# Mixture-of-experts stage of a two-layer encoder: activations turned earlier, the last jobs queued earlier, and row sums with the ones as stationary operand

## The chip, the core and the metric

The kernel runs on one core of one Trainium2 chip. The metric is the device time of one execution in microseconds (us); lower is better. The engines have short names in the profile: PE is the matrix engine (PEld its weight loads), DVE the vector engine, ACT the scalar engine, POOL the general-purpose one, SP the one whose queue issues the weight transfers.

## The reference, cut to what matters

Two trunk layers run on 256 prompt rows and 32 sample rows (288 in all) of width 1024. The change touches only the last step of the second layer: eight experts, of which each row uses two, and the layer norm behind them.

```python
def swiglu(h, wg, wu, wd):
    return (jax.nn.silu(h @ wg) * (h @ wu)) @ wd

def moe_swiglu(h, w_router, wg, wu, wd):
    logits = (h @ w_router).astype(jnp.float32)
    top_val, top_idx = lax.top_k(logits, TOP_K)
    top_w = jax.nn.softmax(top_val, axis=-1)
    combine = jnp.sum(jax.nn.one_hot(top_idx, N_EXPERTS, dtype=jnp.float32) * top_w[..., None], axis=-2)
    out = jnp.zeros_like(h)
    for e in range(N_EXPERTS):          # wg, wu: 1024 x 3584, wd: 3584 x 1024, float32
        out = out + combine[..., e:e + 1] * swiglu(h, wg[e], wu[e], wd[e])
    return out
...
f = moe_swiglu(h, W['w_router'][i], W['w_exp_gate'][i], W['w_exp_up'][i], W['w_exp_down'][i])
x = layer_norm(ALPHA * x + g2 * f, W['ln_g'][l, 1], W['ln_b'][l, 1])
```

## The kernel before, in words

The experts are sorted by the number of their rows (rank r, 0 the fullest). Four are HEAVY (ranks 0, 2, 1, 3 in this order) and four LIGHT (5, 4, 6, 7). A heavy expert has a block of 128 rows (kind "F", computed in three products of a high and a low float32r part); ranks 0 and 1 also have a block of 32 (kind "N", plain float32). A light expert has only an N block, of 64 rows for rank 4 and of 32 for the others. Every expert is worked in four pieces of its 3584 hidden columns (1024, 1024, 1024, 512), and each piece has three phases: `gate`, `up` and `down`. Pieces are counted over all experts of a stream, 0 to 15, so heavy piece 15 is the last of rank 3 and light piece 15 the last of rank 7. The list `phases` fixes one order of all 96 phases, heavy and light in turn; within a stream it goes gate of piece i, down of piece i - 1, up of piece i. Five light phases stand at the end: up of 14, gate of 15, down of 14, up of 15, down of 15.

Weights come in units of 1 MB through a ring of nine buffers (`raw`), in the order of the phases; a transfer is issued by SP as soon as its buffer is given back (L134). For F blocks each half of a unit is split: ACT casts it to `whi` (L158), DVE subtracts to `wlo` (L162). N blocks read `raw` directly, with stationary tiles of 32 or 64 columns, four or two side by side on the array.

Phases touch three PSUM banks named `gu`. A gate or up phase of an F piece takes one for each 512 columns, that of a light N piece takes one, and a bank is free again when the Silu (L1410, L1438) or the product (L1412, L1440) has read it. The N block of a heavy expert uses the bank `ex` instead. `turn` transposes the finished activations of a piece on PE into `gu` banks (L1462) and copies them out, as `hFh` (ACT, L1466) and `hFl` (DVE, L1467) for F, as `tNH` or `tNL` for N (L1335, by ACT and DVE in alternation). `down` multiplies them with the down weights (F: L1490, N: L1510).

Small jobs are Python generators in a list `work`; `filler()` runs one step of the first. They are called after each unit of a light phase, after each unit of an F-only down, and once after each phase. The jobs are `fetch` and `place` (the rows of the next expert), `scatter` (the weighted result of an expert back to all 288 rows, eight steps, L1548 on PE and L1315 on DVE into `xT`), and for the end `gates` (the norm's weights and the gate of the last expert's rows, L1568 to L1579) and `rows`. `rows` first forms the row sums of `xT` (L1591), then `row` transposes `xT` to natural order into the banks of the base (L1607). `before`, called ahead of the very last unit, runs what is left in `work` and does the last two `row`; `finish` adds the last expert and does the layer norm and the stores.

Of the kernel before, what the change touches and what calls it, by code (L numbers as in the profile page):

```python
# [8 lines left out]
F32 = mybir.dt.float32  # L9
# [8 lines left out]
P = 128  # L18
# [189 lines left out]
def body(tc, I, O, CST):  # L208
# [1109 lines left out]
    def experts():  # L1318
        with tc.tile_pool(name="msplit", bufs=4) as ms_pool, tc.tile_pool(name="mw", bufs=2) as mw, \
# [63 lines left out]
            def up(name, stream, at):  # L1383


                r, (c0, n) = stream[at]
                units = n * D // (2048 * P)
                per = 2048 // n
                both = len(UNITS[r]) > 1
                for i, (kind, _, m) in enumerate(UNITS[r]):  # L1390
                    if kind == "F":
                        pss = [gu() for _ in range(n // 512)]
                        xh, xl = X[r, i]
                        for h in range(units):
                            for g in range(2):
                                hi, lo = mring.get((name, r, c0, h), g, AHEAD)
                                for k in range(per // 2):
                                    kk = per * h + per // 2 * g + k
                                    for o, (x, w) in enumerate(((xh, hi), (xl, hi), (xh, lo))):
                                        for c, ps in enumerate(pss):  # L1400
                                            TE.matmul(ps, x[:, kk, :], w[:, k, 512 * c:512 * (c + 1)], start=kk + o == 0,  # L1401
                                                      stop=kk == KT - 1 and o == 2)
                            if not both:
                                ahead()
                        if name == "gate":
                            H[r, c0, i] = mw.tile([P, 1024], F32, name="sg")[:, 0:n]
                        for c, ps in enumerate(pss):
                            d = H[r, c0, i][:, 512 * c:512 * (c + 1)]
                            if name == "gate":
                                S.activation(d, ps, AF.Silu)  # L1410
                            else:
                                V.tensor_mul(d, d, ps)  # L1412
                        continue
                    wd = n * m // P
                    if not both:
                        ps = gu()[:, 0:wd]
                    else:
                        if name == "gate":
                            H["ex"] = acc("ex")
                        ps = H["ex"][:, 0:wd] if name == "gate" else H["ex"][:, wd:2 * wd]  # L1420
                    for h in range(units):
                        w = mring.held((name, r, c0, h)) if both else mring.get_raw((name, r, c0, h))
                        for k in range(per):
                            kk = per * h + k
                            for g in range(P // m):
                                TE.matmul(ps[g * m:(g + 1) * m, :], X[r, i][:, kk, :], w[:, k, g * wd:(g + 1) * wd],  # L1426
                                          start=kk == 0, stop=kk == KT - 1)
                        if both:
                            mring.done_held((name, r, c0, h))
                        else:  # L1430
                            mring.done_raw()
                        ahead()
                        if not both:
                            filler()
                    if name == "gate":
                        d = mw.tile([P, 256], F32, name="hNH") if both else mw.tile([P, 512], F32, name="hNL")
                        H[r, c0, i] = d = d[:, 0:wd]
                        S.activation(d, ps, AF.Silu)  # L1438
                    else:
                        V.tensor_mul(H[r, c0, i], H[r, c0, i], ps)  # L1440
# [32 lines left out]
            def down(stream, at):  # L1473
# [8 lines left out]
                for i, (kind, _, m) in enumerate(UNITS[r]):  # L1482
                    if kind == "F":
                        for h in range(units):
                            for g in range(2):
                                q = 2 * h + g
                                hi, lo = mring.get(("down", r, c0, h), g, AHEAD)
                                for o, (x, w) in enumerate(((hs[i][0], hi), (hs[i][1], hi), (hs[i][0], lo))):
                                    for c in range(2):
                                        TE.matmul(DN[r, i][c], x[:, q, :], w[:, 0, 512 * c:512 * (c + 1)], start=first and q + o == 0,  # L1490
                                                  stop=final and q == 2 * units - 1 and o == 2)
                            if not both:
                                ahead()
                                filler()
                        continue
                    wd = n * m // P
                    nu = max(wd // 256, 1)
                    for h in range(units):
                        if final and r == LIGHT[-1] and h == units - 1:
                            before()  # L1500
                        w = mring.held(("down", r, c0, h)) if both else mring.get_raw(("down", r, c0, h))
                        for k in range(2):
                            if wd == P:
                                x = hs[i][:, m * (2 * h + k):m * (2 * h + k) + m]
                            else:
                                a = P * (2 * (h % nu) + k) + m * (h // nu)
                                x = hs[i][:, a:a + m]
                            for c in range(2):
                                a = 64 * c + k * m % 64
                                TE.matmul(DN[r, i][0][a:a + m, :], x, w[:, k, 512 * c:512 * (c + 1)],  # L1510
                                          start=first and h == 0 and k * m < 64, stop=final and h == units - 1 and (2 - k) * m <= 64)
                        if both:
                            mring.done_held(("down", r, c0, h))
                        else:
                            mring.done_raw()
                        ahead()
                        filler()
                if final and r == LIGHT[-1]:
                    finish(*W.pop((r, 0)), DN[r, 0][0])
                elif final:  # L1520
# [14 lines left out]
                        ys.append((kind, yh, yl, back))  # L1535
                    work.append(scatter(ys))
                    if len(W) == 1 and LIGHT[-1] == next(iter(W))[0]:
                        work.extend((gates(), rows()))

            def scatter(ys):  # L1540
                yield
# [42 lines left out]
            def rows():  # L1584

                st = last["st"] = mw.tile([P, 20], F32, name="stats", bufs=1)
                t = gu()
                for b in (0, 2, 1):
                    t0, n = BLK[b]
                    for k in range(KT):  # L1590
                        TE.matmul(t[0:n, b:b + 1], xT[:, k, t0:t0 + n], ones[:, 0:1], start=b + k == 0, stop=b == 1 and k == KT - 1)  # L1591
                    if b != 1:
                        yield
                V.tensor_scalar(st[:, 16:18], t[:, 0:2], -1.0, None, op0=ALU.mult)
                V.tensor_scalar(st[0:NSA, 18:19], t[0:NSA, 2:3], -1.0, None, op0=ALU.mult)
                yield
                tags = iter(("dF0", "dF1", "dNH", "ex"))
                for b, (t0, n) in enumerate(BLK[:2]):
                    for c in range(2):
                        base[b, c] = acc(next(tags))  # L1600
                        row(b, c)
                        yield

            def row(b, c):
                t0, n = BLK[b]
# [74 lines left out]
            placing = {r: place(r) for r in (HEAVY[0], LIGHT[0])}  # L1680
            following = {**dict(zip(HEAVY, HEAVY[1:])), **dict(zip(LIGHT, LIGHT[1:]))}
            mring.split_to(2)
            for stream, name, at in phases:
                r, c = stream[at]
                if name == "down":
                    turn(stream, at)
                    down(stream, at)
                else:
                    if name == "gate" and c[0] == 0:
                        run_all(placing.pop(r))  # L1690
                    up(name, stream, at)
                filler()
                nxt = following.get(r)
                if nxt is not None and name == "up":
                    if c == PIECES[-2]:
                        work.append(fetch(nxt))
                    elif c == PIECES[-1]:
                        placing[nxt] = place(nxt)
                        work.append(placing[nxt])

    def dense():

# [109 lines left out]
```

## Time and profile before

| | us |
|---|---|
| median of three runs | 1861.44 (1860.39 to 1862.31) |
| the profiled execution, its own time | 1866.27 |
| its span, first to last instruction | 1864.5 |
| PE busy in it | 1743.5 (94%) |
| DVE busy | 1017.8 (55%) |
| ACT busy | 790.6 (42%) |

In the span 525.91 MB go through the DMA queues, 506.76 MB of them through SP's. A share of busy time is a mean over stages with different limits; which engine ends a stage is read from that stage. A DMA share of 1.00 or slightly more in a stretch means that all 16 DMA engines were busy throughout. The granted clock (PEclk) of 1.00 is 2.4 GHz, 0.50 is 1.2 GHz.

### The profile page before, as it was taken

The numbers are of one execution on the slowest core, as the hardware profiler recorded it, in microseconds if no ns is written. First come the engines' busy times: TensorE is split into PE (matmuls) and PEld (weight loads), VectorE is DVE, ScalarE is ACT, GpSimd is POOL, SyncE is SP. The second block draws the span as 40 slices with busy tenths as digits, with TensorE's granted clock in tenths as the row PEclk, the third lists the DMA queues.
The fourth block names the chain that finished last, engine by engine and source line by source line (L and its number), as shares of the span: only waits on it lengthen the run. The fifth ranks groups of instructions, "written<-read, shape, count | busy, mean of one in ns | idle before, by whom it ended". The sixth has DMA issues, their size and how long they took to land. (4 is left out here: it accounts for less than half of the span.)

```text
span 1864.5 us, 31193 instructions
## 1 busy us (share of the span) xinstructions
PE 1743.5 (94%) x12510; PEld 1353.1 (73%) x12510; DVE 1017.8 (55%) x1713; ACT 790.6 (42%) x1230; POOL 140.3 (8%) x176
## 2 busy tenths in 40 slices
PE   7999999899997999998799999999999998999885
PEld 4898889799996988896566665666666665676544
DVE  3446666644445556566445455755555654676432
ACT  1544454434434444453344434445344433454321
POOL 1400100400005101001200000000000000000000
PEclk9999999999998999989799999999999999999896
DMA  9665564685445455631889999999978899999992
GB/s 312 214 216 194 188 206 137 211 276 192 159 158 174 150 194 207 199 131 50 310 338 410 397 399 403 366 381 412 397 297 318 341 403 399 401 411 413 409 409 101
DMA packets 211831, 525.91 MB, mean 282 GB/s; under 512 B 9405, under 2 KB 113062, under 8 KB 198626
## 3 DMA queue, kind: packets, MB, share of 16 engines
q1 hardware_dynamic: 205588, 506.76, 72.7%
q0 software_dynamic: 5680, 16.44, 2.5%
q8 instruction: 100, 1.64, 0.4%
q10 hardware_dynamic: 414, 0.66, 0.1%
q14 instruction: 49, 0.40, 0.1%
HBM read 514.54 MB, written 9.30 MB: 281 GB/s over the span
## 5 line engine op out<-in xcount | busy, mean ns | idle before, releaser
L162 DVE TENSOR_TENSOR wlo<-raw,whi 128x1024 fp32r<-128x1024 f32 x532 | 631.6, 1219 | 305.4 <-ACT whi L158 291.0
L158 ACT CAST whi<-raw 128x1024 fp32r<-128x1024 f32 x532 | 539.1, 1044 | 347.2 <-DMA raw<-in_w_exp_up 78.5
L570 PE MATMUL mm<-hh,whi 128*128 128x288 f32 x888 | 278.2, 313 | 0.8 <-ACT uF L866 0.8
L572 PE MATMUL mm<-hh,wlo 128*128 128x288 f32 x888 | 265.1, 299 | 1.2 <-DVE wlo L162 1.2
L571 PE MATMUL mm<-hl,whi 128*128 128x288 f32 x888 | 265.5, 299 | 0.0
L570 PEld LDWEIGHTS mm<-hh,whi 128*128 128x128 f32 x888 | 169.0, 190 | 24.6 <-issue 14.8
L572 PEld LDWEIGHTS mm<-hh,wlo 128*128 128x128 f32 x888 | 168.6, 190 | 1.9 <-DVE wlo L162 1.9
L571 PEld LDWEIGHTS mm<-hl,whi 128*128 128x128 f32 x888 | 169.2, 190 | 0.3
L1426 PE MATMUL gu<-raw,xNL 128*32 128x256 f32 (+3 forms) x1792 | 137.9, 393 | 4.2 <-DMA raw<-in_w_exp_gate 1.8
L1401 PE MATMUL gu<-whi,xFM 128*128 128x512 f32 x448 | 130.2, 406 | 5.5 <-ACT whi L158 3.2
L1401 PE MATMUL gu<-whi,xFH 128*128 128x512 f32 x448 | 130.6, 407 | 0.9 <-DVE xT L1315 0.8
L1401 PEld LDWEIGHTS gu<-whi,xFM 128*128 128x128 f32 x448 | 85.1, 193 | 33.8 <-issue 6.5
L1401 PEld LDWEIGHTS gu<-whi,xFH 128*128 128x128 f32 x448 | 85.2, 193 | 28.7 <-issue 6.3
L1426 PEld LDWEIGHTS gu<-raw,xNL 128*32 128x32 f32 (+1 forms) x1792 | 63.2, 117 | 58.8 <-issue 30.1
L1490 PE MATMUL dF<-whi,hFh 128*128 128x512 f32 x224 | 76.7, 425 | 8.9 <-ACT hFh L1466 8.8
L1510 PE MATMUL dNL<-raw,tNL 128*32 128x512 f32 (+1 forms) x448 | 67.6, 607 | 13.9 <-DVE tNL L1335 7.8
L1490 PE MATMUL dF<-whi,hFl 128*128 128x512 f32 x224 | 76.9, 427 | 3.8 <-DVE hFl L1467 3.6
L1401 PE MATMUL gu<-wlo,xFM 128*128 128x512 f32 x224 | 75.1, 405 | 0.6 <-DVE wlo L162 0.5
L1401 PE MATMUL gu<-wlo,xFH 128*128 128x512 f32 x224 | 74.6, 403 | 0.0
L1490 PE MATMUL dF<-wlo,hFh 128*128 128x512 f32 x224 | 73.8, 412 | 0.0
L571 PE MATMUL lg<-hl,whi 128*128 128x288 f32 x216 | 64.5, 298 | 0.0
L572 PE MATMUL lg<-hh,wlo 128*128 128x288 f32 x216 | 64.2, 297 | 0.0
(505 smaller groups left out, 2688.8 us busy)
## 6 DMA issues: line engine op xcount, KB each, us to landing
raw<-in_w_exp_gate SPq DMA_DIRECT2D x112, 1024.0 KB, 12.8
raw<-in_w_exp_up SPq DMA_DIRECT2D x112, 1024.0 KB, 12.0
raw<-in_w_exp_down SPq DMA_DIRECT2D x112, 1024.0 KB, 13.9
raw<-in_w_ada SPq DMA_DIRECT2D x48, 1024.0 KB, 7.4
raw<-in_w_in SPq DMA_DIRECT2D x44, 1024.0 KB, 5.6
raw<-in_w_ffn_gate SPq DMA_DIRECT2D x11, 1024.0 KB, 5.1
raw<-in_w_ffn_up SPq DMA_DIRECT2D x11, 1024.0 KB, 7.7
raw<-in_w_attn_up SPq DMA_DIRECT2D x8, 1024.0 KB, 6.7
```

Source lines behind the costliest of these rows:

```text
L158: self.nc.scalar.copy(hv, raw)
L162: eng.tensor_sub(lv, raw, hv.bitcast(F32))
L570: TE.matmul(ps, hi[:, s[0], s[1]], xh, start=first, stop=False)
L571: TE.matmul(ps, hi[:, s[0], s[1]], xl, start=False, stop=False)
L572: TE.matmul(ps, lo[:, s[0], s[1]], xh, start=False, stop=last)
L1401: TE.matmul(ps, x[:, kk, :], w[:, k, 512 * c:512 * (c + 1)], start=kk + o == 0, stop=kk == KT - 1 and o == 2)
L1426: TE.matmul(ps[g * m:(g + 1) * m, :], X[r, i][:, kk, :], w[:, k, g * wd:(g + 1) * wd], start=kk == 0, stop=kk == KT - 1)
L1490: TE.matmul(DN[r, i][c], x[:, q, :], w[:, 0, 512 * c:512 * (c + 1)], start=first and q + o == 0, stop=final and q == 2 * units - 1 and o == 2)
L1510: TE.matmul(DN[r, i][0][a:a + m, :], x, w[:, k, 512 * c:512 * (c + 1)], start=first and h == 0 and k * m < 64, stop=final and h == units - ...
```

## The change

Four edits, all within the expert stage. `turn` is no longer called at the start of a down phase but up to two phases ahead of it, as soon as the piece's up phase is behind (for most pieces, directly behind the gate phase of the next piece of its stream). `gates` is queued behind the up phase of the last heavy piece instead of behind the last scatter. While only one block is left to be scattered (`len(W) == 1`), two fillers run per light unit. The row sums take the ones as stationary operand (32 columns, four tiles side by side) and `xT` as the moving one; three small products then add up the four partial sums; `row(0, 0)` stands between.

```diff
@@ up(), a light N piece, after each unit (and the same in down())
                         if not both:
                             filler()
+                            if len(W) == 1:
+                                filler()
@@ down(), behind the scatter of a heavy expert
                     if len(W) == 1 and LIGHT[-1] == next(iter(W))[0]:
-                        work.extend((gates(), rows()))
+                        work.append(rows())
@@ rows()
                 st = last["st"] = mw.tile([P, 20], F32, name="stats", bufs=1)
                 t = gu()
+                for k in range(KT):
+                    g = k % 4
+                    TE.matmul(t[32 * g:32 * g + 32, 0:T], ones[:, 0:32], xT[:, k, :], start=k < 4, stop=k >= 4)
+                sums = mw.tile([P, 1024], F32, name="sg")[:, 0:T]
+                S.copy(sums, t[:, 0:T])
+                yield
+                tags = iter(("dF0", "dF1", "dNH", "ex"))
+                base[0, 0] = acc(next(tags))
+                row(0, 0)
+                yield
+                t = gu()
                 for b in (0, 2, 1):
                     t0, n = BLK[b]
-                    for k in range(KT):
-                        TE.matmul(t[0:n, b:b + 1], xT[:, k, t0:t0 + n], ones[:, 0:1], start=b + k == 0, stop=b == 1 and k == KT - 1)
-                    if b != 1:
-                        yield
+                    TE.matmul(t[0:n, b:b + 1], sums[:, t0:t0 + n], cst[:, C_COMB:C_COMB + 1], start=b == 0, stop=b == 1)
                 V.tensor_scalar(st[:, 16:18], t[:, 0:2], -1.0, None, op0=ALU.mult)
                 V.tensor_scalar(st[0:NSA, 18:19], t[0:NSA, 2:3], -1.0, None, op0=ALU.mult)
-                yield
-                tags = iter(("dF0", "dF1", "dNH", "ex"))
-                for b, (t0, n) in enumerate(BLK[:2]):
-                    for c in range(2):
-                        base[b, c] = acc(next(tags))
-                        row(b, c)
-                        yield
+                for b, c in ((0, 1), (1, 0), (1, 1)):
+                    base[b, c] = acc(next(tags))
+                    row(b, c)
+                    yield
@@ the loop over the phases
-            for stream, name, at in phases:
+            turned = set()
+            for i, (stream, name, at) in enumerate(phases):
                 r, c = stream[at]
                 if name == "down":
-                    turn(stream, at)
                     down(stream, at)
...
+                if stream is heavy and name == "up" and at == len(heavy) - 1:
+                    work.append(gates())
+                for s, what, j in phases[i + 1:i + 3]:
+                    if what == "down" and s[j] not in turned and (s, "up", j) not in phases[i + 1:i + 3]:
+                        turned.add(s[j])
+                        turn(s, j)
```

**Place 1: PE, in the second heavy expert (rank 2).** PE's order before, from the gate phase of light piece 6 (`raw`, stationary `xNL`) over the transposes of heavy piece 5 to its down phase:

```order
L1401 MATMUL gu<-wlo,xFM_10793 128x512 x2
L1426 MATMUL gu<-raw_9011,xNL 64x512 x4
L1426 MATMUL gu<-raw_9012,xNL 64x512 x4
L1426 MATMUL gu<-raw_60,xNL 64x512 x4
L1426 MATMUL gu<-raw_61,xNL 64x512 x4
L1462 MATMUL gu<-cst,sg 128x128 x8
L1490 MATMUL dF_11390<-whi,hFh 128x512
L1490 MATMUL dF_11391<-whi,hFh 128x512
```

PE's order of the change at the same place (line 1464 is the transpose, 1492 the down product):

```order
L1401 MATMUL gu<-wlo,xFM_10793 128x512 x2
L1464 MATMUL gu<-cst,sg 128x128 x8
L1426 MATMUL gu<-raw_9011,xNL 64x512 x4
L1426 MATMUL gu<-raw_9012,xNL 64x512 x4
L1426 MATMUL gu<-raw_60,xNL 64x512 x4
L1426 MATMUL gu<-raw_61,xNL 64x512 x4
L1492 MATMUL dF_11390<-whi,hFh 128x512
L1492 MATMUL dF_11391<-whi,hFh 128x512
```

The eight transposes have moved from between the light gate phase and the heavy down phase to directly behind the heavy phase; four light units now lie between them and the products that read them.

**Place 2: PE, the last weights.** PE's order before, from the last unit of down of light piece 14 on (`raw_9012` and `raw_60` are the two units of up of piece 15, `raw_61` and, behind these rows, `raw_62` those of its down):

```order
L1510 MATMUL dNL<-raw_9011,tNL 32x512 x4
L1579 MATMUL gu<-xFM_15740,xFM_15741 64x512 x2
L1591 MATMUL gu<-ones,xT 128x1 x8
L1426 MATMUL gu<-raw_9012,xNL 32x128 x16
L1591 MATMUL gu<-ones,xT 32x1 x8
L1426 MATMUL gu<-raw_60,xNL 32x128 x16
L1591 MATMUL gu<-ones,xT 128x1 x8
L1607 MATMUL dF_15837<-cst,xT 128x128 x4
L1462 MATMUL gu<-cst,hNL 128x128
L1510 MATMUL dNL<-raw_61,tNL 32x512 x4
L1607 MATMUL dF_15850<-cst,xT 128x128 x4
L1607 MATMUL dNH<-cst,xT 128x128 x4
```

PE's order of the change, first the gate phase of light piece 15 (its units are `raw_62` and `raw_63`) with the new row sums (1594, 1605) and the rows (1616):

```order
L1594 MATMUL gu<-xT,ones 32x288 x8
L1464 MATMUL gu<-cst,hNL 128x128 x2
L1426 MATMUL gu<-raw_62,xNL 32x128 x16
L1616 MATMUL dF_15753<-cst,xT 128x128 x4
L1605 MATMUL gu<-cst,sg 128x1
L1605 MATMUL gu<-cst,sg 32x1
L1605 MATMUL gu<-cst,sg 128x1
L1616 MATMUL dF_15764<-cst,xT 128x128 x4
L1426 MATMUL gu<-raw_63,xNL 32x128 x16
L1616 MATMUL dNH<-cst,xT 128x128 x4
L1616 MATMUL ex<-cst,xT 128x128 x4
```

and then, directly behind these (three like the first of these rows stand between), the last weights:

```order
L1512 MATMUL dNL<-raw_9011,tNL 32x512 x4
L1426 MATMUL gu<-raw_9012,xNL 32x128 x16
L1426 MATMUL gu<-raw_60,xNL 32x128 x16
L1464 MATMUL gu<-cst,hNL 128x128
L1512 MATMUL dNL<-raw_61,tNL 32x512 x4
L1616 MATMUL gu<-cst,xT 32x128 x8
L1512 MATMUL dNL<-raw_62,tNL 32x512 x4
```

The last product of `gates`, the row sums and the four rows of the prompt have moved from behind the down phase of piece 14 to ahead of it; the rows of the sample (32x128) have stayed.

**Place 3: ACT, the last heavy piece.** ACT's order before, from the Silu of light gate phase 14 on (`raw_60` and `raw_9009`, `raw_9010` are weights of heavy piece 15; `hFh` is the copy for its down phase):

```order
L1438 ACTIVATE hNL<-gu 128x256
L158 CAST whi<-raw_60 128x1024 x2
L158 CAST whi<-raw_9009 128x1024 x2
L1466 CAST hFh<-gu 128x512
L158 CAST whi<-raw_9010 128x1024 x2
L1532 ACTIVATE yhF<-dF_14612,wFM 128x512
L1532 ACTIVATE yhF<-dF_14613,wFM 128x512
```

ACT's order of the change there (`xFM` are the tiles in which `gates` keeps its operands):

```order
L1440 ACTIVATE hNL<-gu 128x256
L158 CAST whi<-raw_60 128x1024 x2
L1468 CAST hFh<-gu 128x512
L1335 COPY xFM_15554<-gu 2x512
L158 CAST whi<-raw_9009 128x1024 x2
L1335 COPY xFM_15555<-gu 2x128
L158 CAST whi<-raw_9010 128x1024 x2
L1536 ACTIVATE yhF<-dF_14612,wFM 128x512
L1536 ACTIVATE yhF<-dF_14613,wFM 128x512
```

The copy `hFh` has moved ahead of the cast of the down weights `raw_9009`; a small copy of `gates` now stands behind that cast.

## Rows read from the trace of the kernel before

**Rows 1.** The page, 40 equal slices of 46.6 us, DMA engines' busy share in tenths.

```profile
DMA  9665564685445455631889999999978899999992
```

**Rows 2.** Busy time by stretch (us): PE, PEld, DVE, ACT, POOL, then PEclk, DMA share, GB/s.

```profile
1180.00:1350.00 170.00, 166.84 (x766) 104.47 (x763) 98.19 (x121) 76.64 (x89) 2.69 (x3) 0.99 1.00 389
1350.00:1510.00 160.00, 155.71 (x1127) 100.05 (x1127) 88.89 (x112) 70.33 (x83) 0.00 (x0) 1.00 0.84 329
1510.00:1780.00 270.00, 249.08 (x1767) 171.10 (x1767) 153.49 (x181) 120.70 (x140) 2.98 (x4) 0.95 1.02 407
1780.00:1820.00 40.00, 31.69 (x271) 17.02 (x269) 15.03 (x30) 6.86 (x10) 0.00 (x0) 0.96 1.02 408
```

**Rows 3.** Chain that ended last, 1819 us to the last down product: start, length, what.

```profile
1819.52 1.00 PE gu L1579 x4
1820.52 2.31 PE gu L1591 x16
1822.83 1.84 PE gu L1426 x30
1824.68 0.75 PE gu L1591 x14
...
1827.24 3.50 PE gu L1591 x16
1830.74 1.92 PE dF L1607 x8
...
1833.25 1.94 PE dNL L1510 x8
1835.19 2.01 PE dF L1607 x8
1837.20 1.71 PE dNH L1607 x8
1838.90 0.93 PE ex L1607 x8
1839.83 1.76 PE gu L1607 x15
1841.59 1.06 PE dNL L1510 x6
```

**Rows 4.** Busy time by stretch around the last landing and from there to the end.

```profile
1820.00:1843.00 23.00, 22.17 (x181) 18.07 (x177) 0.96 (x5) 2.07 (x3) 0.00 (x0) 0.63 0.29 114
...
1827.00:1828.00 1.00, 1.00 (x9) 0.84 (x5) 0.00 (x0) 0.00 (x0) 0.00 (x0) 0.50 0.30 123
1828.00:1829.00 1.00, 1.00 (x6) 1.00 (x6) 0.00 (x0) 0.00 (x0) 0.00 (x0) 0.50 0.02 8
```

**Rows 5.** PE's timeline, 1180 to 1510 us: idle before a group, and its releaser.

```profile
1179.20 1.06 PE L1510 MATMUL dNL<-raw,tNL 128*32 128x512 f32 x8 [0.35 <-ACT tNL L1335]
...
1239.70 7.09 PE L1510 MATMUL dNL<-raw,tNL 128*64 128x512 f32 x32 [1.27 <-DVE tNL L1335]
...
1425.65 3.65 PE L1510 MATMUL dNL<-raw,tNL 128*64 128x512 f32 x16 [0.46 <-ACT tNL L1335]
```

**Rows 6.** The same view elsewhere: two waits behind ACT, one light unit, one row sum.

```profile
1546.08 0.70 PE L1462 MATMUL gu<-cst,hNH 128*128 128x128 f32 x2 [2.65 <-ACT hNL L1438]
...
1792.84 0.73 PE L1490 MATMUL dF<-whi,hFh 128*128 128x512 f32 x2 [3.44 <-ACT hFh L1466]
...
1801.29 1.07 PE L1426 MATMUL gu<-raw,xNL 128*32 128x256 f32 x16
...
1843.74 0.85 PE L1631 MATMUL gu<-stats,bkNL 128*128 128x1 f32 x6 [1.19 <-DVE stats L1626]
```

**Rows 7.** ACT's timeline: a cast that waited for its weights, and a Silu of a gate.

```profile
1420.96 1.08 ACT L1410 ACTIVATE sg<-gu 128x512 f32<-128x512 f32 x2 [4.77 <-PE gu L1401]
...
1790.31 1.99 ACT L158 CAST whi<-raw 128x1024 fp32r<-128x1024 f32 x2 [10.54 <-DMA raw<-in_w_exp_down]
```

**Rows 8.** Busy time in a stretch with a fall of the clock.

```profile
1040.00:1050.00 10.00, 9.49 (x29) 7.24 (x28) 7.60 (x9) 6.34 (x8) 0.00 (x0) 0.66 1.01 417
```

More of the change, by code (lines that the diff above doesn't have):

```diff
@@ L1517, in down @@
                         filler()
+                        if len(W) == 1:
+                            filler()
                 if final and r == LIGHT[-1]:
```

## The prediction

> **What bounds the kernel now.** I read the page first, its row of the DMA engines: they are full in the last half of the span, apart from slices 29 to 32 (1305 to 1491 us), and idle in the last one [rows 1]. So the expert stage is a stream of weights with one thin place and a tail, and the three want different arguments. The busy times by stretch give the thin place: between 1350 and 1510 us the DMA share is 0.84 while PE is busy 155.71 of 160 us. PE paces there, and buffers are given back too late. Between 1180 and 1350 us PE (166.84 of 170) and the stream (1.00) run neck and neck; I count this stretch as paced by PE too, since what PE loses there it lacks at 1350. From 1510 to 1820 us the share is 1.02 and PE has idle time, 8.31 of 40 us in 1780 to 1820 [rows 2]. The stream paces there: a wait of PE costs nothing, but where the stream stands at 1510 us decides when the last weights land.
>
> Then the chain that ended last. From 1819.52 us to the end of the last product of down, 1841.59 + 1.06 = 1842.65 us, it lies on PE almost without a gap [rows 3], while the DMA share falls to 0.30 at 1827 and to 0.02 at 1828 us [rows 4]. The last weights are there at 1828.0 us, and PE needs 14.65 us more. Behind it come `finish` and the stores, 1842.65 to 1864.5 us, 21.9 us, which the change leaves as they are.
>
> So there are two terms: PE's work behind the last weights, and PE's idle time between 1180 and 1510 us.
>
> **Term 1, the end.** Of the 23.1 us between 1819.52 and 1842.65 us the change moves ahead: the last product of `gates` 1.00, the row sums 2.31 + 0.75 + 3.50 = 6.56, and four rows 1.92 + 2.01 + 1.71 + 0.93 = 6.57, together 14.13 us [rows 3]. What stays is 9.0 us: two units of up (1.84, and one like it), transposes and copy, a unit of down 1.94, the sample's rows 1.76, the last unit 1.06. PE alone would end at 1842.65 - 14.13 = 1828.5 us.
>
> The weights do not allow that. At 408 GB/s [rows 2] a unit of 1.05 MB takes 2.57 us, so the last four, two of up and two of down, land at about 1820.3, 1822.9, 1825.4 and 1828.0 us. In the kernel before, the mean clock of this stretch is 0.63 although PE is busy 22.17 of 23 us, and 0.50 around 1828 us [rows 4]; the rows above are mostly at the lower level. Two values follow.
> - At 2.4 GHz throughout only the last unit counts: 1828.0 + 1.06 = 1829.1 us, a gain of 13.5 us.
> - At 1.2 GHz the chain starts at the second unit of up: 1822.9 + 1.84, product, transposes and copy about 1.1 (of which 0.6 is the step from 1830.74 + 1.92 to 1833.25 us [rows 3]; the rest is my estimate) makes 1825.8; + 1.94 = 1827.8; + 1.76 = 1829.5; + 1.94 = 1831.5 us, a gain of 11.2 us.
>
> I take the lower clock, since it is the nearest row: the same small products in the same place ran at it. In the changed kernel PE also waits for each of the last units. The Trainium skill, "TensorE: Matmul & The Clock Gate", Part 1, says that the engine's clock is halved after idling and comes back with sustained work; by that the tail would be at half, 11.2 us, and the trace agrees with the level but not with idling as the only cause, because PE was busy when it fell.
>
> Does the moved work fit ahead of 1820 us? At full clock it is four rows at 0.93 [rows 3], 3.7 us, the `gates` product 1.0, and the new row sums. The trace has none of these; the nearest row is a light unit, eight products of 32 columns with 256 moving: 1.07 us [rows 6], for 288 columns 1.2 us. The three small ones behind them are like the three products of line 1631, 0.85 us [rows 6]. Together 6.8 us into 8.3 us of idle time [rows 2]. The largest piece of that idle time is the wait of 3.44 us at 1792.84 us [rows 6], and only `gates` can use it. There I expect no gain for PE: its `hFh` copy is now ahead of the cast that waited 10.54 us for its weights [rows 7], but a small copy of `gates` is behind that cast, which ends at 1790.31 + 1.99 = 1792.3 us, and PE's last `gates` product waits for it; with a copy of about 0.3 and the product's 1.0 us PE goes on at 1793.6 instead of 1792.84 us. Behind that, 8.3 - 3.4 = 4.9 us of idle time take rows and sums of 5.8 us, while the other steps of `gates` leave the stretch. So PE reaches the last units at best on time and at worst some 2 us late; I put 0.5 us. The two sums and products of `finish` on PE may run at the lower clock: 0.5 us more. ACT's new copy of the sums (128x288) has a row's transpose beside it and costs nothing; alone it would be some 0.4 us. Scatter steps in pairs change when, not how much.
>
> Term 1: 11.2 - 0.5 - 0.5, **10 us**; between 13.5 (full clock, on time) and 7 (lower clock, 2 us late and a slower `finish` by 1).
>
> **Term 2, the turns.** The transposes are not fewer. What they cost before is PE's wait behind them for the copies. Between 1180 and 1510 us the timeline has eight such waits, the first 0.35, the longest 1.27, the last 0.46 [rows 5]; the other five are 0.20, 0.70, 0.20, 0.68 and 0.68, sum 4.54 us. All go, as light units now lie between transposes and down (place 1). Such waits ahead of 1180 and behind 1510 us lie where the stream paces, and I count nothing for them.
>
> New waits can come from the three `gu` banks. Directly behind the gate of an F-only piece (three places in this stretch) two banks still hold that gate, and the second group of transposes needs the first of them: it waits for a Silu of 1.08 / 2 = 0.54 us [rows 7], largely under the first four transposes. In rank 1 (three places) the light gate behind the turn needs a bank which the copies `hFh` and `hFl` have to release first. No row shows this; from nothing to 1.27 us each, the longest wait for a copy [rows 5]. I take 0.35, near the shortest of these, because transposes run meanwhile: 2.0 us for six.
>
> Term 2: 4.5 - 2.0, **2.5 us** of gain; between 4.5 and a loss of 3.1 (six at 1.27).
>
> **Sum.** 10 + 2.5 = 12.5 us. The profiled execution would take 1866.27 - 12.5 = 1853.8 us; it lies 4.8 us over the median, and the terms are the same for both, so the median of runs goes from 1861.44 to **1849 us**, 0.7% less.
>
> **The rivals.**
> - *All of it.* The clock holds at the end, and no bank wait comes: 13.5 + 4.5 = 18 us, 1843.4 us. For it: PE will be nearly gapless until 1818 us. Against: it was so before, and the clock fell.
> - *The end does not fit.* The idle time ahead of 1820 us [rows 2] is waits for single units, and work put between two units may only delay the next. Then just what got smaller is saved: row sums from 6.56 to 1.2 + 0.85 us, 4.5 us, and term 2 between 0 and 2.5: 1854.4 to 1857 us.
> - *Slower, by the clock.* In rank 1's pieces the change puts the N block, the transposes, the light gate and its transposes together, a run of small tiles without a dense block. If the clock fell in these runs, where PE paces: a stretch of 10 us with a fall has 0.66 [rows 8], which costs 3.4 us. Five falls (17 us) use up the 12.5 us and 0.2% more; six, one for each heavy piece between 1180 and 1510 us, give 1849 + 20.4 = 1869 us. The rule that would do it is in the Trainium skill, "TensorE: Matmul & The Clock Gate", Part 1. Against: PE ran at 0.99 and 1.00 there [rows 2], with small tiles in long runs already.
> - *A Silu behind a waiting cast.* Where ACT stands in a cast that waits for weights, a bank comes late: the trace has 2.65 us for it [rows 6]. At the three F-only places that is 8 us; with an end that does not fit, 4.5 - 8 + 4.5, nothing is left: about 1861 us.
>
> **How the numbers follow.** My forecast (1845.5 to 1853 us): 0.58. All of it: 0.17. The end does not fit: 0.15. Nothing left: 0.04. The clock: 0.06. A measurement can tell about 0.2%, 3.7 us, from no change. Faster by more than that are the first three, with little of them lost at the edge: 0.88; within it 0.05; slower 0.07. For the range I go down to 1842 us, a little below the second case, and up to 1857 us, the end of the third; the last two cases stay out.
>
> **What would show it.** Right: PE's last product about 10 us nearer to the last landing; no wait of a down product for `hFh` or `tNL`; the DMA share between 1350 and 1510 us up by one to three hundredths. Wrong: PE waiting for `gu` banks behind the turns (Silu, `hFl`); the clock at 0.50 between 1350 and 1510 us; the last weights landing later than before, measured from the stream's start; or PE still at row sums or rows when the last unit has landed.

## The result

The changed kernel takes 1840.26 us (median of four runs, 1836.77 to 1846.03) against 1860.91 us (1857.85 to 1862.31) of the kernel before, run beside it: ratio 0.9891, 95% interval 0.9864 to 0.9917. That is 20.6 us less. Forecast were 12.5 us less, 1849 us with a range of 1842 to 1857: the direction is right, and the time lies below the range. A second set of six runs of the changed kernel gave 0.9897 (0.9874 to 0.9919).

The profiled execution of the changed kernel has a span of 1839.7 us and a time of its own of 1841.58 us. Its DMA row on the page answers to [rows 1]: the last slice has 4 instead of 2 tenths, and the thin place is a little shallower (one slice with 8 instead of 7).

```profile
DMA  9665564686445465632689999999988899999994
```

Busy time by stretch, to be read beside [rows 2] and [rows 4]: the DMA share in 1350 to 1510 us is 0.90 (it was 0.84; the same time is not quite the same place of the program, since the changed kernel is ahead there), and the last weights land at 1813.0 us (before: 1828.35 us).

```profile
1180.00:1350.00 170.00, 168.46 (x827) 106.47 (x827) 93.37 (x112) 75.29 (x88) 3.44 (x3) 1.00 0.98 387
1350.00:1510.00 160.00, 157.03 (x1163) 101.56 (x1163) 92.42 (x118) 68.64 (x79) 0.00 (x0) 0.99 0.90 351
1510.00:1780.00 270.00, 244.56 (x1693) 166.42 (x1693) 152.53 (x179) 121.20 (x142) 2.98 (x4) 0.94 1.02 409
...
1811.00:1812.00 1.00, 0.71 (x4) 0.23 (x8) 0.00 (x0) 0.00 (x0) 0.00 (x0) 0.50 0.12 49
1812.00:1813.00 1.00, 1.00 (x9) 0.21 (x2) 0.00 (x0) 0.00 (x0) 0.00 (x0) 0.50 0.08 33
1813.00:1814.00 1.00, 1.00 (x9) 0.85 (x5) 0.00 (x0) 0.00 (x0) 0.00 (x0) 0.50 0.00 0
```

The chain that ended last, where [rows 3] had twelve pieces of PE: one transfer, a unit of down, the sample's rows, the last unit.

```profile
1792.35 18.80 DMA raw<-in_w_exp_down
1811.15 0.14 issue
1811.29 1.93 PE dNL L1512 x8
1813.22 3.15 PE gu L1616 x15
1816.37 1.50 PE dNL L1512 x6
```

Where the time went is told by three marks in each profile: the first product of a light expert (PE's line 1426, 909.79 us before and 905.22 us now), the last landing, and the end of the last product of down (1842.65 and 1817.87 us).

| | before | after | difference |
|---|---|---|---|
| first light product | 909.8 | 905.2 | -4.6 |
| from there to the last landing | 918.6 | 907.8 | -10.8 |
| from there to the last product of down | 14.3 | 4.9 | -9.4 |
| from there to the end of the span | 21.9 | 21.8 | 0 |

The first line lies ahead of all that was changed. The 18 profiles of this study have this mark between 904.2 and 909.8 us, with and without the change (904.6 in `c3_again`, where only the end differs from before; 909.2 in `c2_pad_late`, which has the whole change), so it is taken as scatter; its cause is open. The second is the turns, forecast at 2.5 us; the third is the end, forecast at 10 us. The experiments below take the two apart.

The busy times between the first light product and the first product of rank 4 (the expert with 64 rows) show how PE came to be earlier in the stream. Before, and then after:

```profile
909.79:1154.34 244.55, 234.10 (x1906) 159.37 (x1906) 126.33 (x136) 108.41 (x132) 1.88 (x2) 0.96 0.99 390
```

```profile
905.22:1142.75 237.53, 229.68 (x1905) 157.06 (x1905) 126.73 (x136) 108.63 (x131) 2.77 (x2) 0.97 0.99 392
```

The same products (a record is missing) take 7.0 us less, all of it ahead of 1180 us: 2.6 us less idle (10.45 to 7.85) and 4.4 us less busy. Most of the 4.4 us is the clock, which was at 0.50 for 14.2 us of this stretch instead of 21.1; but that time scatters, and `c4_again`, with the old turns and 13.8 us, is busy for 231.21 us, so some 1.5 us are not the clock. The gain itself is steady: seven profiles with the old turns take 243.1 to 245.1 us for this stretch, seven with all the early turns of the change 236.5 to 237.5 us. One place where the clock fell before, PE's timeline at the second turn of rank 0, before:

```profile
1039.12 0.51 PE L1462 MATMUL gu<-cst,hNH 128*128 128x128 f32 x2 [1.58 <-ACT hNL L1438]
1039.60 0.78 PE L1490 MATMUL dF<-whi,hFh 128*128 128x512 f32 x2
1040.89 1.22 PE L1490 MATMUL dF<-whi,hFl 128*128 128x512 f32 x2 [0.51 <-DVE hFl L1467]
1041.91 1.05 PE L1490 MATMUL dF<-wlo,hFh 128*128 128x512 f32 x2
```

and after (the timeline, then a window of this stretch):

```profile
1036.48 0.71 PE L1492 MATMUL dF<-whi,hFh 128*128 128x512 f32 x2
1037.02 0.62 PE L1492 MATMUL dF<-whi,hFl 128*128 128x512 f32 x2
1037.48 0.63 PE L1492 MATMUL dF<-wlo,hFh 128*128 128x512 f32 x2
...
1034.50:1044.50 10.00, 10.00 (x73) 7.52 (x62) 9.00 (x9) 6.56 (x8) 0.00 (x0) 1.00 1.01 417
```

Before, PE waits 1.58 and 0.51 us, and the pairs of products behind take 0.78, 1.22 and 1.05 us; after, there is no wait, and they take 0.71, 0.62 and 0.63 us. The stretch had a granted clock of 0.66 [rows 8]; now it has 1.00.

### The profile page after: what moved, and what is told of

The parts are those of the page before. It is cut to its first block, busy times and chain, and to the rows that moved or that the text cites. A ratio compares the mean times of both kernels' runs of the same rounds, so it can differ in the third digit from the quotient of the medians.

```text
span 1839.7 us, 31125 instructions
## 1 busy us (share of the span) xinstructions
PE 1722.1 (94%) x12484; PEld 1338.3 (73%) x12484; DVE 1017.9 (55%) x1713; ACT 790.8 (43%) x1231; POOL 143.3 (8%) x176
## 5 line engine op out<-in xcount | busy, mean ns | idle before, releaser
L1492 PE MATMUL dF<-whi,hFl 128*128 128x512 f32 x224 | 73.2, 409 | 0.0
## 6 DMA issues: line engine op xcount, KB each, us to landing
raw<-in_w_exp_gate SPq DMA_DIRECT2D x112, 1024.0 KB, 14.3
raw<-in_w_exp_down SPq DMA_DIRECT2D x112, 1024.0 KB, 14.3
```

## The experiments

A saving in us is one minus the ratio, times the 1860.9 us of before.

**Which turns, and where.** Theory W: PE sets the pace from the first light product to 1500 us, and its position there is what counts, though the DMA engines are full. Theory P is the prediction's: where they are full, PE's time costs nothing. Five kernels have the last hunk of the change without the rest; `a1_turns_only` has all of it, the others one condition more, and a piece that is not turned ahead is turned at the start of its down phase as before.

```diff
+                for s, what, j in phases[i + 1:i + 3]:
-                    if what == "down" and s[j] not in turned and ...
+                    if what == "down" and j < 4 and s[j] not in turned and ...       # a3_turns_first
+                    if what == "down" and j >= 4 and s[j] not in turned and ...      # a4_turns_rest
+                    if what == "down" and s is heavy and s[j] not in turned and ...  # b2_turns_heavy
+                    if what == "down" and s is light and s[j] not in turned and ...  # b3_turns_light
```

`a1_turns_only`: 

> The kernel before with the turns ahead and nothing else of the change. Theory W (PE paces from the start of the expert stage to about 1500 us, so every wait and every fall of the clock there counts, whether the DMA engines are full or not): 12 to 13 us less than before. Theory P (the prediction: only waits between 1180 and 1510 us count): about 2.5 us less.

`a3_turns_first`: 

> Turns ahead for the pieces 0 to 3 of both streams alone (the first heavy and the first light expert, up to about 1150 us), nothing else of the change. W: 6 to 7 us less than before, since the first product of rank 4 lies 7.0 us earlier in the changed kernel, counted from the stage's start, and what PE has gained there the stream keeps. P: no change, since the DMA engines are full there before.

`a4_turns_rest`: 

> Turns ahead for the pieces 4 to 15 alone. W: 5 to 6 us less than before, together with the first pieces as much as all turns. P: 2.5 us less, as much as all turns.

`b2_turns_heavy`: 

> The kernel before with only the heavy pieces' activations turned ahead. Of PE's waits at turns between 960 and 1154 us in the kernel before, eight with 6.8 us lie at heavy downs (waits for the Silu and product of hNL, and for hFh and hFl) and three with 1.6 us at light ones; the clock's falls at 1040 and 1142 us begin with waits at heavy downs. Theory W with these shares: 9 to 11 us faster than the kernel before. If the light turns carry the gain, 2 to 4 us.

`b3_turns_light`: 

> The kernel before with only the light pieces' activations turned ahead. Theory W with the shares of the waits: 2 to 3 us faster than the kernel before. If the light turns carry the gain: 8 us or more.

The last two columns are from each kernel's profile: from the first light product to the first product of rank 4, and to the last landing (before: 244.6 and 918.6 us).

| kernel | ratio | 95% interval | saving, us | to rank 4, us | to the last landing, us |
|---|---|---|---|---|---|
| a1_turns_only | 0.9942 | 0.9920 to 0.9964 | 10.8 | 236.5 | 906.9 |
| a3_turns_first | 0.9965 | 0.9947 to 0.9983 | 6.5 | 237.2 | 911.1 |
| a4_turns_rest | 0.9979 | 0.9959 to 0.9999 | 3.9 | 243.6 | 912.6 |
| b2_turns_heavy | 0.9939 | 0.9916 to 0.9962 | 11.3 | 237.5 | 907.5 |
| b3_turns_light | 0.9984 | 0.9967 to 1.0001 | 3.0 | 241.3 | 915.2 |

The two parts by place add up to the whole (6.5 + 3.9 against 10.8). The landings, of one profile each, tell the same: in `a3_turns_first` PE is 7.4 us earlier at rank 4, and the last weights land 7.4 us earlier, so what PE gains there the stream keeps to its end. Pieces 0 to 3 are those of the first heavy and the first light expert, all turned ahead of 1155 us; by theory P they are worth nothing, and they are worth 6.5 us. Between its first light product and the first product of rank 4 this kernel takes 237.20 us like the changed one:

```profile
908.10:1145.30 237.20, 229.68 (x1906) 157.16 (x1906) 126.76 (x136) 108.58 (x131) 2.76 (x2) 0.97 0.99 392
```

The heavy turns carry the gain, as the waits had it; alone they are worth as much as all turns. The light ones' 3 us can by their interval also be nothing, and the two together come to more than the whole (11.3 + 3.0 against 10.8), which the intervals allow.

**The end: sums or moves.** `a2_end_only` is the change without that hunk, `c3_sums_only` the kernel before with nothing but the new sums (the hunk in `rows`), `c4_moves_only` is `a2_end_only` with the old sums. The last two were run twice.

`a2_end_only`: 

> The change without the turns ahead: gates queued earlier, two fillers a unit, new row sums. Both theories: the time from the last landing to the last down product falls from 14.7 us to 6 to 7 us, 8 us less than before, and the stream before it stays as it was. If the two halves of the change need each other, less.

`c3_sums_only`: 

> The kernel before with only the new row sums (ones as the stationary operand, row(0, 0) between sums and their totals); gates, rows and turns stay where they were. Counted from rows: sums 6.56 us at the lower clock become about 1.9 us at the higher level or 3.8 us at the lower, and all of it still lies behind 1820 us on PE: 3 to 4.5 us faster than the kernel before. If the end's gain of the whole change came from the smaller sums alone: 8 us faster. If the move ahead makes all of it: no change.

`c3_again`: 

> The kernel before with only the new row sums, once more: 7 to 9 us faster than the kernel before if the sums alone carry the end's gain, 3 to 4.5 us if they save only their own time.

`c4_moves_only`: 

> The kernel before with the small jobs of the end queued earlier and two per unit, the row sums as before (one moving column per product), turns as before. Theory S (the sums with one moving column lie just ahead of the clock's fall and cause it; the new sums carry the end's gain): the clock falls to 0.50 behind these sums, now earlier, and PE is behind the last landing by several us again; at most 4 us faster than the kernel before. Theory M (moving the work off the tail carries the gain, as the prediction had it): 6 to 9 us faster, as with both.

`c4_again`: 

> The kernel before with the small jobs of the end queued earlier and two per unit, the row sums as before, once more beside the sums alone. Its first profile has 7.7 us from the last landing to the last product of down against 14.2 us before, its first median only 0.9 us less than before. If the profile speaks for all runs: 6 us faster than the kernel before. If the median does: 0 to 3 us faster, and the move ahead is worth next to nothing without the new sums.

| kernel | ratio | 95% interval | saving, us | last landing to last product of down, us |
|---|---|---|---|---|
| a2_end_only | 0.9959 | 0.9942 to 0.9975 | 7.6 | 2 |
| c3_sums_only | 0.9957 | 0.9934 to 0.9981 | 8.0 | 5 |
| c3_again | 0.9965 | 0.9949 to 0.9981 | 6.5 | 4 |
| c4_moves_only | 0.9991 | 0.9971 to 1.0011 | 1.7 | 8 |
| c4_again | 0.9985 | 0.9969 to 1.0002 | 2.8 | 9 |

The new sums alone give as much as the whole end (8.0 and 6.5 us against 7.6); the moves alone are worth 1.7 and 2.8 us, and both intervals hold zero. Up to the last landing these five profiles take 915.9 to 919.2 us (before: 918.6), so the end's edits act behind it. The sums' own time was expected at 3 to 4.5 us, and the intervals of both runs hold this too; that the rest is the clock is read from the profiles. In the kernel before, PE has run at the sums (line 1591) since 1820.52 us [rows 3], and the clock falls, although PE is busy throughout:

```profile
1820.00:1822.00 2.00, 2.00 (x17) 1.55 (x14) 0.00 (x0) 1.39 (x2) 0.00 (x0) 0.95 1.03 391
1822.00:1824.00 2.00, 2.00 (x28) 1.90 (x32) 0.00 (x0) 0.68 (x2) 0.00 (x0) 0.50 1.05 415
```

In `c4_again` the old sums (line 1595 there) start 12 us sooner, at 1808.55 us, and the fall moves with them (timeline of PE, then windows):

```profile
1808.55 1.92 PE L1595 MATMUL gu<-ones,xT 128*128 128x1 f32 x16 [0.56 <-DVE xT L1315]
1810.39 1.40 PE L1426 MATMUL gu<-raw,xNL 128*32 128x128 f32 x32
1811.55 4.51 PE L1595 MATMUL gu<-ones,xT 128*32 128x1 f32 x32
...
1808.00:1810.00 2.00, 1.45 (x14) 1.48 (x14) 1.28 (x5) 0.00 (x0) 0.00 (x0) 1.00 1.00 414
1810.00:1812.00 2.00, 2.00 (x46) 1.94 (x46) 0.00 (x0) 0.00 (x0) 0.00 (x0) 0.75 1.00 414
1812.00:1814.00 2.00, 2.00 (x18) 1.99 (x17) 0.00 (x0) 0.00 (x0) 0.00 (x0) 0.50 1.04 411
```

In `c3_again` the new sums stand where the old ones stood, and the clock holds to the last product of down; sums, unit and rows take 1.2, 1.1 and 1.2 us:

```profile
1814.34 1.18 PE L1590 MATMUL gu<-xT,ones 128*32 128x288 f32 x16
1815.34 1.06 PE L1426 MATMUL gu<-raw,xNL 128*32 128x128 f32 x32
1816.32 1.16 PE L1612 MATMUL dF<-cst,xT 128*128 128x128 f32 x8
...
1820.00:1822.00 2.00, 1.62 (x19) 1.38 (x18) 0.32 (x2) 0.00 (x0) 0.00 (x0) 1.00 0.80 317
1822.00:1823.00 1.00, 1.00 (x9) 0.16 (x9) 0.00 (x0) 0.00 (x0) 0.00 (x0) 1.00 0.10 33
1823.00:1824.00 1.00, 1.00 (x12) 0.93 (x8) 0.00 (x0) 0.00 (x0) 0.00 (x0) 1.00 0.00 0
1824.00:1826.00 2.00, 2.00 (x22) 1.88 (x24) 0.00 (x0) 0.00 (x0) 0.00 (x0) 1.00 0.00 0
```

All profiles go this way. In the eight with the old sums the clock falls between 0.0 and 2.8 us behind the start of the first sum and stays at 0.50 for 3.4 to 17.1 us; in the ten with the new sums no fall begins within 14 us behind their start. (In the changed kernel it falls 16.8 us behind them, after the wait of 1.53 us at the last up unit.) What starts the fall is still open: in `a1_turns_only` it begins together with the first sum, not behind it. No profile has more than the 17.1 us of the kernel before, so that profile shows the end at its worst.

The Trainium skill, "TensorE: Matmul & The Clock Gate", Part 1, puts the lower clock down to an idle engine. At 1039.12 us of the kernel before this agrees in kind (waits of 1.58 and 0.51 us lie ahead of the slow products); at the sums it does not, if idle is read from the profile's busy time: PE is busy 2.00 of 2.00 us.

**PE's time, early and late.** Here work is added to the changed kernel: each group of a heavy piece's transposes is done three times, in pieces 0 to 3 (`c1_pad_early`) or 10 to 13 (`c2_pad_late`), or the first four products of each gate and up phase of the first light expert five times (`d1_pad_light`).

```diff
+                        for _ in range(3 if kind == "F" and at < 4 else 1):       # c1; c2: 9 < at < 14
                             for q, x in enumerate(part):
...
+                            for e in range(5 if kk == 0 and r == LIGHT[0] else 1):    # d1
                                 for g in range(P // m):
...
```

`c1_pad_early`: 

> The changed kernel with each group of transposes of heavy pieces 0 to 3 done three times (the output is unchanged): 56 more transposes at 0.154 us, 8.6 us more of PE work, all of it ahead of 1140 us, where the profile shows the DMA engines full. Theory W (PE paces from the start of the expert stage to 1510 us, so PE time counts there in full): 8 to 9 us slower than the changed kernel, about 1849 us. Theory P (the one of the prediction: where the DMA engines are full the stream paces, and PE time costs nothing): within 2 us of the changed kernel, about 1840 us.

`c2_pad_late`: 

> The same 56 more transposes, 8.6 us, in heavy pieces 10 to 13, between 1520 and 1735 us, where the changed kernel's PE has 26 us of idle time and waits for weights. Both theories: the stream paces there, 0 to 2 us slower than the changed kernel. If PE time counted everywhere in the stage: 8 to 9 us slower.

`d1_pad_light`: 

> The changed kernel with the first four products of every gate and up phase of the first light expert (rank 5) done five times: 128 more products, 96 of 0.067 and 32 of 0.034 us, 7.5 us more of PE work between 905 and 1140 us, in a place where PE does not wait for copies. Theory W: the last weights land 6 to 8 us later, measured from the start of the expert stage, and the time is 6 to 8 us over the changed kernel. Theory P: no later, within 2 us of the changed kernel.

The ratios are 0.9906 (0.9877 to 0.9934), 0.9876 (0.9850 to 0.9902) and 0.9923 (0.9899 to 0.9948), against 0.9891 and 0.9897 of the changed kernel. So `c2_pad_late` costs nothing, `c1_pad_early` some 2 us (0.0009 to 0.0015 of 1860.9) and `d1_pad_light` 4.8 us (0.0026, against the changed kernel on the same chip); the intervals of the last two overlap that of the changed kernel. Both early ones miss what theory W said; `d1_pad_light` misses theory P's 2 us as well. The windows up to rank 4 tell why, `c1_pad_early` and then `d1_pad_light`:

```profile
905.35:1144.18 238.83, 234.13 (x1962) 162.45 (x1962) 126.90 (x136) 108.64 (x131) 2.82 (x2) 0.98 0.99 392
```

```profile
904.21:1144.98 240.77, 237.65 (x2162) 163.12 (x2162) 126.44 (x136) 108.53 (x132) 2.90 (x2) 0.98 0.99 391
```

PE is busy 4.5 and 8.0 us longer than in the changed kernel, but idle 3.1 and 4.7 us less (4.70 and 3.12 instead of 7.85 us): extra work runs where PE had waited for copies and casts. (The clock was also low for less time, 10.9 and 8.2 us instead of 14.2, so these figures mix two things; of the 8.6 us forecast for the pad of `c1_pad_early`, 4.5 show as busy time.) What is left, 1.3 and 3.2 us, is how much later PE reaches rank 4, and about what the times show; the last weights of `d1_pad_light` land 911.2 us behind the first light product, 3.4 and 4.5 us later than in the two profiles of the changed kernel. Theory W holds for PE's position, not for each us of PE's work.

**The sample's rows earlier.** The chain of the changed kernel has 3.15 us of these rows behind the wait for the last piece's first down unit. One edit puts them ahead of it.

```diff
-                        if final and r == LIGHT[-1] and h == units - 1:
+                        if final and r == LIGHT[-1] and h == 0:
                             before()
```

`b1_sample_rows`: 

> The changed kernel with the last two row() (the sample's rows, 3.15 us at the lower clock) ahead of the wait for the last piece's first down unit (1.55 us) instead of ahead of the second, whose weights have landed by then. If PE's work behind the last landing sets the end: 1.5 to 3 us faster than the changed kernel, about 1838 us. If those weights' landing or the finish behind it sets it: no change.

`b1_again`: 

> The changed kernel with the sample's rows ahead of the wait for the last piece's first down unit, once more beside the changed kernel itself. By the profiles, 1.6 instead of 4.8 us from the last landing to the last product of down: 3 us faster than the changed kernel. If the difference between the two profiles is chance: no change.

`after_again`: 

> The changed kernel itself, for the comparison with the sample's rows moved and with the extra products: 1838 to 1844 us.

The first gave 1840.0 us, 0.9887 (0.9859 to 0.9914); the second 1838.53 us, 0.9887 (0.9863 to 0.9912), beside 1841.26 us, 0.9897 (0.9874 to 0.9919), of the changed kernel. PE's timeline of `b1_again` has the rows in the former wait, and its last down unit ends at 1813.71 us, some 2 us behind the last landing:

```profile
1809.52 2.36 PE L1616 MATMUL gu<-cst,xT 128*32 128x128 f32 x15
1811.62 0.63 PE L1512 MATMUL dNL<-raw,tNL 128*32 128x512 f32 x3
1811.72 0.27 PE L1616 MATMUL gu<-cst,xT 128*32 128x128 f32 x1
1811.83 1.88 PE L1512 MATMUL dNL<-raw,tNL 128*32 128x512 f32 x13
```

This is the lowest median of the study (the lowest ratio is that of `c2_pad_late`); that it beats the changed kernel (by 0.7 to 1.9 us, from the ratios) is not shown, since the intervals overlap.

## Why the prediction was right or wrong

- **The step that failed** is in term 2: "Such waits ahead of 1180 and behind 1510 us lie where the stream paces, and I count nothing for them." Forecast were 2.5 us from the turns; alone they gave 10.8 us, and 6.5 us came from pieces all turned ahead of 1155 us. The step took a DMA share near 1.00 as proof that PE cannot delay the stream. The rate says otherwise. Counted from the first light product, the first 400 us and the next 200 us of the kernel before, of the changed kernel and of `a3_turns_first`:

```profile
909.79:1309.79 400.00, 386.33 (x2577) 252.22 (x2577) 219.95 (x253) 177.62 (x208) 2.82 (x3) 0.97 0.99 389
1309.79:1509.79 200.00, 195.42 (x1331) 126.30 (x1330) 109.50 (x138) 87.19 (x103) 1.75 (x2) 0.99 0.88 342
...
905.22:1305.22 400.00, 391.12 (x2624) 257.28 (x2625) 227.44 (x261) 185.02 (x216) 5.34 (x4) 0.98 1.00 397
1305.22:1505.22 200.00, 196.16 (x1356) 127.92 (x1359) 111.19 (x139) 84.88 (x101) 0.87 (x1) 0.99 0.89 349
...
908.10:1308.10 400.00, 389.07 (x2611) 254.75 (x2612) 223.57 (x258) 181.85 (x214) 4.57 (x4) 0.98 1.00 396
1308.10:1508.10 200.00, 195.62 (x1328) 127.64 (x1327) 113.23 (x140) 88.41 (x104) 0.87 (x1) 0.99 0.88 343
```

Where the stream paces, behind 1510 us, it moves 407 GB/s [rows 2]. At a share of 0.99 it moved 389: not at its own level, and late buffers from PE could slow it. The 8 GB/s that the changed kernel gains over the first 400 us are 3.2 MB, 7.9 us at 407 GB/s; the thin place adds 7 x 200 = 1.4 MB, 3.4 us. Together they are about the 10.8 us of the earlier landing, and `a3_turns_first` has its gain almost all in the first 400 us. The hint was in the row: 389 GB/s beside a share of 1.00 between 1180 and 1350 us [rows 2]. (The share of 0.90 for 0.84 in 1350 to 1510 us makes the thin place look like the main part; at the same place of the program it is 0.89 for 0.88.) Behind 1510 us the count of nothing fits (`c2_pad_late`).
- **Left out** was the clock as a gain. The third rival had more falls of the clock as a loss; up to rank 4 the profile of the changed kernel has 6.9 us less at 0.50. At 1039 us the wait ahead of the fall is gone as well; that the waits are the cause is argued from that place, not isolated by a run. Of the 7.0 us that PE gained up to rank 4, 4.4 are busy time.
- **Term 1** had the right size: 10 us, measured 7.6 alone and 9.4 in the profile, inside 7 to 13.5. That was partly luck, since its mechanism, the move, is not what saved the time. It counted 14.13 us of work moved ahead and took the lower clock as given, because "the same small products in the same place ran at it". But in the kernel before the old sums came ahead of that fall, and with the new sums there the clock of all that stands behind them holds too; the moves alone gave 1.7 and 2.8 us, not clear of nothing.
- **Smaller steps.** Term 2's own parts came out: from 1180 to 1510 us no down product waits for `hFh` or `tNL` any more, and the waits for `gu` banks are 1.9 us where 2.0 had been put (0.68 and 0.46 behind `tNL`, 0.72 behind `tNH`). The new sums were put at 1.2 and 0.85 us; in the changed kernel they take 1.2 and 0.7 us. PE reached the last units in time: it waits 1.53 and 1.55 us for the last up unit and the first down unit. `finish` takes no longer (21.8 us). That `gates` would wait for a copy behind a waiting cast came true: 2.23 us at 1775.83 us, where PE had time.

```profile
1775.83 1.67 PE L1583 MATMUL gu<-xFM,xFM 2*64 2x512 f32 x4 [2.23 <-ACT xFM L1335]
...
1807.85 1.08 PE L1426 MATMUL gu<-raw,xNL 128*32 128x128 f32 x32 [1.53 <-DMA raw<-in_w_exp_up]
...
1811.29 1.93 PE L1512 MATMUL dNL<-raw,tNL 128*32 128x512 f32 x8 [1.55 <-DMA raw<-in_w_exp_down]
```

- **The rivals.** "All of it" named 1843.4 us and came nearest, by luck: its condition, the clock holding at the end, is not met (the sample's rows still take 3.15 us at 0.50), and its 4.5 us for the turns were too few. "The end does not fit" had one thing right, that moving the work saves little by itself, but it put the smaller sums at 4.5 us, and `a2_end_only` gave 7.6. That the clock would cost, and that a Silu would wait, are refuted by the sign and size of `a1_turns_only`.

## What to carry to other kernels

A DMA share near 1.00 does not show that the stream paces: put the rate beside the highest rate of the same kernel (here 389 beside 407 GB/s), and look at what PE waits for. From 905 to 1350 us of the kernel before PE waits for copies and casts and never for weights, and there its delay went into the stream. A wait can cost more than its length, when the products behind it run at the lower clock; look at the mean time of the same products behind it. Row sums with the ones as the stationary operand and many moving columns were the better form here: with the ones as the moving operand each profile had the clock down from the sums on.

## What the runs showed of the hardware

- The granted clock fell from 1.00 to 0.50 while PE was busy 2.00 of 2.00 us with products of one moving column, in two places 12 us apart in time, and held at 1.00 where products with 288 columns did the same sums. What starts the fall is not settled (`a1_turns_only`).
- A stretch with a DMA share of 0.99 moved 389 GB/s, one with 1.02 in the same kernel 407 GB/s; PE's earlier turns alone brought the first to 396 to 398 GB/s (`a3_turns_first`, `a1_turns_only`).
- Added PE work in a stretch with 7.85 us of idle time took up 3.1 us of it in one case and 4.7 us in the other, so that 8.0 us more of busy time made PE only 3.2 us later.
- The first light product lies between 904.2 and 909.8 us in 18 profiles of kernels that do not differ ahead of it; why is open.
